# A hybrid decoder layer on one core: three token chunks in the first phase, value products of a chunk as one batch, masks in pairs

## The chip, the cores and the metric

The kernel runs on one core of a Trainium2 chip. The metric is the device time of one execution in microseconds (us); smaller is better. The core has a matrix engine (PE in the profile, with PEld for its weight loads), a vector engine (DVE), a scalar engine (ACT), a general engine (POOL), and a queue engine that issues most DMAs (SP). Matrix products land in eight banks of PSUM of 128 partitions by 512 floats; everything else lives in SBUF or in DRAM.

## The reference

One layer over a prompt of 2048 tokens (width 1024) and over 8 single-token decode requests. From the normalised input one projection of 3592 columns gives q, k, v (8 heads of 64), a forget gate per head, a gate za, and u, gv, zc of the spatial-gating group. Cut to what matters:

```python
h = rms_norm(x, g_norm);  p = h @ w_in
q, k, v, fz, za, u, gv, zc = split(p)          # q, k also RMS-normed per head
c = cumsum(log_sigmoid(fz + b_f))
s = q @ k.T * SCALE + c[t] - c[s]              # causal: s <= t, else -inf
attn = softmax(s) @ v
mix = tril(W_s) @ rms_norm(gv) + b_s           # inside chunks of 128 positions
y = x + concat(attn * silu(za), u * mix * silu(zc)) @ w_out
```

k, v and the log gates of the prompt are outputs too. The decode requests read paged caches of 512 positions. Products are in fp32 precision: most factors are split into a high and a low part of the reduced format fp32r, and three products (high*high, high*low, low*high) are summed.

## The kernel before

**First phase** (up to about 588 us). The prompt's normalised input is transposed and split; chunk `cp` of 512 tokens is four tiles of 2048 floats (`hh`, `hl`, 16 tiles over four chunks, from the pool `big` with 16 places). Eight units of weights follow each other. Units 0 to 4 (q, k, v, gates, gv) go over all 16 token tiles. Units 5 to 7 hold the weights of u, zc and za; they go over the first `NCP` chunks only, with two features at a time into the `acc` banks, 24 products of 512 columns for each feature and chunk. Meanwhile the decode requests' cache pages are read and scored. During unit 7 the first of the row maxima below are already made.

**Second phase** (to about 1169 us). `UNITS` is the list of (head h, chunk c of 512 queries). For each unit, `values` makes the transposed scores of every key tile kt of 128 keys (4c+4 of them): a product with `k1` (128 rows: high and low parts of k), one with `k2` (68 rows), both into a bank `sc`; the four tiles on the diagonal get a causal mask by a bf16 product of `identb` and `maskb` into the same bank between the two. ACT takes the exponential into a place `p` of `ring`; POOL (and DVE for some) adds the tiles up into `acc` for the softmax sum. The value products (`av` from `p` and `vst`, true fp32, 64 columns of the array, even key tiles in one half and odd ones in the other) are queued in `avq` and run when eight key tiles have been done (`AVB`) or the unit ends. A unit with c = 3 so has two batches of eight. At the end the two halves of `av` are added, stored (`aT`), and later `add_up` transposes the sums.

For a head, `maxima` runs ahead: products of `q1` and `k2` into banks `tp`, for each query tile i in pieces of up to 512 keys, the last piece with the same kind of mask product, then a DVE minimum (`mn`) of each piece. `load_queries` brings a unit's queries (`q2`) in five DMAs, six key tiles before the unit before it ends (`QLEAD`).

Between these, `fill` hands out *filler*: the u, zc, za products of the chunks that the first phase left out (`filler`, bank `fl`, 24 products a feature and chunk, with new weights from `fill_weights` for each feature), then `load_out_weights` and the output products. The dose is `FILL` times the estimated time of the work just issued, `FILL7` in the last three units. With `FILL` 0.50 the 24 feature-chunks (two chunks of 12 features) last into unit (6,3).

**Last phase**: the remaining output products, into the banks `sc` and `av`.

PE's order is written out by hand in the order of the Python code; `Pe.clock` adds up estimated PE time, and `later(ns, fn)` defers a step until that clock has moved on. The other engines run in the order of the framework's scheduler; each engine and the SP queue is strictly first in, first out. The PSUM banks of the second phase are `sc` 2 (`NSC`), `tp` 3, `av` 2 (`NAV`), `fl` 1; a tile of a tag takes the bank of an earlier tile of that tag, and its first product waits until that one was read out.

Of the kernel before, what the change touches and what calls it, by code (L numbers as in the profile page):

```python
# [19 lines left out]
P = 128  # L20
# [58 lines left out]
def hymba_step(ctx, tc, x_prompt, x_sample, cache_k, cache_v, cache_logf, page_table, g_norm, w_in,  # L79
# [712 lines left out]
    def filler():  # L792
        jobs = [(o + f * P, f) for f in range(4) for o in (OZA, OU, OZC)] if NCP < 4 else []
        nxt = first.pop()
        mxs = {}
        units = []
        for n, (o, f) in enumerate(jobs):
            units.append(nxt)
            if n + 1 < len(jobs):
                nxt = fill_weights(jobs[n + 1][0])  # L800
            if n + 2 >= len(jobs):
                continue
            unit = units.pop()
            while len(unit) < KT:
                yield -1
            for cp in range(NCP, 4):
                if n % 3 == 0:
                    yield from za_steps(unit, 0, f, cp, "fl")
                elif n % 3 == 1:
                    mxs[cp] = s2(t="mxu")  # L810
                    yield from u_steps(unit, 0, f, cp, "fl", mxs[cp])
                else:
                    yield from zc_steps(unit, 0, f, cp, "fl", mxs.pop(cp))
                yield 0
        while min(len(unit) for unit in units) < KT:
            yield -1
        for cp in range(NCP, 4):
            mx = s2(t="mxu")
            yield from u_steps(units[0], 0, f, cp, "fl", mx)
            yield 0  # L820
            yield from zc_steps(units[1], 0, f, cp, "fl", mx)
            if cp == 3:
                break
            yield 0
            while "k1" not in heads.get(NH - 1, {}):
                yield -1
            load_out_weights(0)
# [69 lines left out]
    def maxima(hd):  # L897
# [2 lines left out]
        nxt = qhi.pop() if qhi else load_hi(h, 0)  # L900
        for c in range(2):
            q = nxt
            for i in range(8 * c, 8 * c + 8):
# [4 lines left out]
                cut = pieces((i + 1) * P)  # L908
                if i % 4 == 0:
                    part = sm.tile([P, 4, len(cut)], F32, tag="mn", bufs=3, name=tname("mn"))  # L910
                for n, (c0, m) in enumerate(cut):
                    sp = bank("tp")[:, :m]
                    end = n == len(cut) - 1
                    mm(sp, q[:HD + 2, (i % 8) * P:(i % 8 + 1) * P], hd["k2"][:HD + 2, c0:c0 + m], True, not end,
                       max(m, 256) * 0.422)
                    if end:
                        mm(sp[:, m - P:], identb, maskb[:, 0], False, True, 56)
                    nc.vector.tensor_reduce(part[:, i % 4, n:n + 1], sp, axis=AX.X, op=ALU.min)  # L918
                    yield m * 0.422
                if i % 4 == 3:  # L920
                    shifts(h, i // 4, part)

    shifted = set()
# [22 lines left out]
            later(3500, store)  # L946
        later(SLAG, turn)

    avq = []

    def run_av(keep):
        while len(avq) > keep:
            avq.pop(0)()

    due = {}
    nt = [0]
    qload = {}
# [5 lines left out]
    def values(at):  # L963

        h, c = UNITS[at]
        hd, q, acc, st = heads[h], qload.pop((h, c)), accs[at % 2], {}
        for kt in range(4 * c + 4):
            if kt == max(0, 4 * c + 4 - QLEAD) and at + 1 < len(UNITS):
                qload[UNITS[at + 1]] = load_queries(*UNITS[at + 1])
            n0 = max(0, kt - 4 * c) * P  # L970
            ns = max(512 - n0, 256) * 0.422
            sp = bank("sc")
            ks = slice(kt * P, (kt + 1) * P)
            mm(sp[:, n0:], hd["k1"][:, ks], q[:, n0:512], True, False, ns)
            if kt >= 4 * c:
                mm(sp[:, n0:n0 + P], identb, maskb[:, 1], False, False, 56)
            mm(sp[:, n0:], hd["k2"][:HD + 4, ks], q[:HD + 4, 512 + n0:], False, True, ns)
            if kt == 0:
                flush(at % 2)
            p = ring[nt[0] % len(ring)]  # L980
            nt[0] += 1
            nc.scalar.activation(p[:, n0:], sp[:, n0:], AF.Exp, bias=zero1, scale=-1.0)  # L982
            if kt == 0 or kt == 2 and c:
                p0 = p
            elif kt == 1:
                if n0:
                    nc.gpsimd.memset(p[:, :n0], 0.0)
                    n0 = 0
                nc.gpsimd.tensor_tensor(acc, p0, p, op=ALU.add)
            elif kt == 3 and c:  # L990
                nc.vector.tensor_tensor(accd, p0, p, op=ALU.add)
            elif kt % 4 == 3 and kt < 4 * c:
                nc.vector.tensor_tensor(accd, accd, p, op=ALU.add)
            else:
                nc.gpsimd.tensor_tensor(acc[:, n0:], acc[:, n0:], p[:, n0:], op=ALU.add)  # L995
                if kt == 4 * c + 1:
                    nc.gpsimd.tensor_tensor(acc, acc, accd, op=ALU.add)

            def step(kt=kt, p=p, n0=n0, acc=acc, c=c, st=st, at=at):

                if kt == 0:
                    st["av"] = bank("av")
                av, fin = st["av"], kt == 4 * c + 3
                e = kt % 2
                mm(av[e * HD:(e + 1) * HD, n0:], hd["vst"][:, kt], p[:, n0:], kt < 2, kt >= 4 * c + 2,
                   (512 - n0) * 0.844)
                if fin:
                    t = s2(t="at")
                    nc.scalar.copy(t[:HD], av[HD:])
                    nc.vector.tensor_tensor(t[:HD], t[:HD], av[:HD], op=ALU.add)  # L1010
                    later(STLAG if h < NH - 2 else STLAST, lambda: nc.sync.dma_start(aT[h * HD:(h + 1) * HD, c * 512:(c + 1) * 512], t[:HD]))

                    def add_up():
                        pt = bank("tp")
                        for j in range(4):
                            transpose(pt[:, j * P:(j + 1) * P], acc[:, j * P:(j + 1) * P], ident)
                        rs = small(4)
                        nc.vector.tensor_reduce(rs, pt.rearrange("p (j k) -> p j k", j=4), axis=AX.X, op=ALU.add)
                        nc.vector.reciprocal(rs, rs)

                        def done():
                            pt = bank("tp")
                            transpose(pt[:4, :P], rs, ident)
                            t = s2(t="rt")[:4, :P]
                            nc.scalar.copy(t, pt[:4, :P])

                            def store():
                                nc.sync.dma_start(rT[h, c * 512:(c + 1) * 512].rearrange("(n p) -> n p", p=P), t)
                                if h % 2:
                                    later(STLAST, lambda: gate(h // 2, c))  # L1030
                            later(STLAG if h < NH - 2 else STLAST, store)
                        later(2000, done)
                    due[at % 2] = add_up
                    later(ACLAG, lambda: flush(at % 2, add_up))
            avq.append(step)
            if kt % AVB == AVB - 1 or kt == 4 * c + 3:
                run_av(0)
            yield 2 * ns + (512 - n0) * 0.844

    MT = 17408 * 0.422  # L1040
    VT = 17408 * 0.422 * 4
# [95 lines left out]
    def out_tiles():  # L1137

        gs = None
        for i in range(NT):  # L1140
# [13 lines left out]
                gs = decode_out()  # L1154
            if gs is not None and i < 12:
                next(gs, None)
            yield from out_products(i, **ins.pop(i), tags=("sc", "av") if last_phase[0] else ("fl", "fl"))

    mgen = all_maxima()
    mdone = [0.0]  # L1160
# [111 lines left out]
    for at, (h, c) in enumerate(UNITS):  # L1272
        if c == 0 and h < NH - 1:
            heads[h + 1] = load_keys(h + 1)
        if (h, c) == (DSTART, 0):
            Pe.decode, Pe.steps = Pe.clock, chain(decode_gate(), decode_attention())
        dose = FILL if at < len(UNITS) - 3 else FILL7
        for v in values(at):
            vdone += v
# [2 lines left out]
            while mdone[0] / MT < min(vdone / VT + AHEAD, NH):  # L1282
# [4 lines left out]
                mdone[0] += m  # L1287
                fill(m * dose)
                pump()
    run_av(0)  # L1290
    hold[0] = 0.0
    last_phase[0] = True
    for _ in fgen:
# [39 lines left out]
```

## Time and profile before

| | us |
|---|---|
| median of 3 runs (1343.99 to 1346.61) | 1346.32 |
| profiled execution, its own time | 1347.51 |
| its span, first to last instruction | 1345.8 |
| PE busy, weight loads busy | 1304.6, 1006.6 |
| DVE, POOL, ACT busy | 706.9, 574.6, 433.1 |

Mean granted clock of the matrix engine: 0.987. All products are recorded on one helper line (L174; transposes on L178), so groups are told apart by tile names: `acc` is the first phase, `sc<-q,k` scores, `tp<-k,q` maxima, `av<-p,vst` value products, `fl` filler, `sc<-wo,am` and `av<-wo,am` output. Ends of products are modelled and overlap the next one's start, so the price of a product is read from the distance between starts, not from its listed duration. Each value product of one key tile appears as two records.

### The profile page before, as it was taken

What the parts mean: (1) busy time and instruction counts of PE and PEld (TensorE: products, weight loads), DVE (VectorE), ACT (ScalarE), POOL (GpSimd) and SP (SyncE); (2) the same over time, 40 slices, a digit from 0 to 9 for tenths busy, and PEclk for the clock granted to TensorE, in tenths of its full rate; (3) what the DMA queues carried; (4) which work ended last, traced back from release to release, by engine and by line L of the source; (5) the groups of instructions that cost most, each with busy time, mean ns of one, the idle gap of its engine ahead of it and who ended that gap; (6) DMA issues with size and microseconds to landing.
All of it is one profiled execution on the core that took longest, in us unless ns stands there. A gap on an engine that the chain in (4) does not pass through costs nothing.

```text
span 1345.8 us, 19516 instructions
## 1 busy us (share of the span) xinstructions
PE 1304.6 (97%) x6544; PEld 1006.6 (75%) x6544; DVE 706.9 (53%) x1328; ACT 433.1 (32%) x781; POOL 574.6 (43%) x679
## 2 busy tenths in 40 slices
PE   6999999999999999999999999999999998999998
PEld 5999999999887877866666566666656664688877
DVE  4346654534678544266586555566565774322321
ACT  5542332222222111114453344434444456310100
POOL 3113343423223554416776666676757466400000
PEclk9999999999999999999998899999999998999999
DMA  6644353555113665634254854666375645463221
GB/s 217 188 119 112 87 142 116 155 140 158 52 48 99 187 184 148 159 97 127 78 138 85 181 138 126 177 182 169 95 192 135 172 119 196 135 238 117 107 77 49
DMA packets 170805, 183.09 MB, mean 136 GB/s; under 512 B 39402, under 2 KB 125866, under 8 KB 169138
## 3 DMA queue, kind: packets, MB, share of 16 engines
q1 hardware_dynamic: 166818, 173.08, 46.7%
q10 hardware_dynamic: 3488, 8.39, 1.6%
q8 instruction: 52, 0.85, 0.3%
q14 instruction: 47, 0.39, 0.1%
q0 software_dynamic: 400, 0.38, 0.1%
HBM read 121.53 MB, written 60.28 MB: 135 GB/s over the span
## 4 chain that ended last, share of the span: by engine, by line
PE 85%; DMA 6%; DVE 4%; ACT 2%; issue 1%; SPq 1%; POOL 1%; ACTq 0%; DVEq 0%; POOLq 0%
PE acc L174 36%; PE sc L174 15%; PE av L174 14%; PE fl L174 10%; PE tp L174 5%; PE tp L178 3%; PE pm L174 1%; DVE mn L918 1%; ACT p L982 1%; DMA xp<-in_x_prompt_dram 1%; DMA raw<-in_w_in_dram 1%; DMA q<-qk_hi 1%; DMA k<-qk_lo 1%; DMA q<-qk_lo 1%; DMA mrow<-mt 0%
## 5 line engine op out<-in xcount | busy, mean ns | idle before, releaser
L982 ACT ACTIVATE p<-sc,zero 128x512 f32<-128x512 f32 (+1 forms) x320 | 196.6, 623 | 173.9 <-PE sc L174 167.9
L995 POOL TENSOR_TENSOR acc<-acc,p 128x512 f32<-128x512 f32 (+3 forms) x184 | 194.1, 1055 | 125.2 <-ACT p L982 104.1
L918 DVE TENSOR_REDUCE mn<-tp 128x1 f32<-128x384 f32 (+6 forms) x320 | 186.9, 604 | 107.9 <-PE tp L174 105.6
L174 PE MATMUL acc<-wh,hh 128*128 128x384 f32 (+2 forms) x640 | 228.7, 357 | 0.0
L174 PE MATMUL acc<-wl,hh 128*128 128x384 f32 (+2 forms) x640 | 222.8, 348 | 1.0 <-DVE wl L256 0.9
L174 PE MATMUL acc<-wh,hl 128*128 128x384 f32 (+2 forms) x640 | 222.6, 348 | 0.6 <-DVE hl L248 0.6
L174 PE MATMUL sc<-q,k 128*128 128x512 f32 (+7 forms) x640 | 211.1, 407 | 10.6 <-ACT p L982 5.9
L174 PEld LDWEIGHTS sc<-q,k 128*128 128x128 f32 (+1 forms) x640 | 118.2, 197 | 35.3 <-ACT p L982 16.3
L174 PE MATMUL av<-p,vst 128*64 128x512 f32 (+3 forms) x640 | 135.4, 543 | 0.0
L174 PEld LDWEIGHTS acc<-wh,hh 128*128 128x128 f32 x640 | 120.7, 189 | 7.2 <-ACT hh L243 0.2
L174 PEld LDWEIGHTS acc<-wl,hh 128*128 128x128 f32 x640 | 120.9, 189 | 6.3 <-DVE wl L256 2.0
L174 PEld LDWEIGHTS acc<-wh,hl 128*128 128x128 f32 x640 | 120.3, 188 | 6.3 <-DVE hl L248 1.2
L174 PE MATMUL tp<-k,q 66*128 66x384 f32 (+6 forms) x320 | 120.3, 392 | 3.9 <-DVE mn L918 3.3
L236 POOL TENSOR_SCALAR sm<-sm 128x6 f32<-128x6 f32 (+3 forms) x84 | 20.3, 241 | 238.8 <-DVE sm L389 170.4
L174 PEld LDWEIGHTS av<-p,vst 128*64 128x64 f32 x640 | 47.9, 137 | 67.1 <-issue 57.6
L237 POOL TENSOR_TENSOR sm<-sm,mhalf 128x6 f32<-128x6 f32 (+3 forms) x84 | 89.6, 1067 | 6.7
L174 PE MATMUL sc<-wo,am 128*128 128x512 f32 x360 | 84.5, 390 | 0.0
L174 PE MATMUL av<-wo,am 128*128 128x512 f32 x360 | 84.2, 389 | 0.0
L174 PEld LDWEIGHTS tp<-k,q 66*128 66x128 f32 x320 | 61.2, 193 | 26.6 <-DVE mn L918 6.6
L174 PE MATMUL acc<-hh,wh 128*128 128x512 f32 x192 | 76.3, 397 | 4.9 <-DVE s L378 4.9
L174 PEld LDWEIGHTS av<-wo,am 128*128 128x128 f32 x360 | 67.5, 188 | 14.2
L174 PEld LDWEIGHTS sc<-wo,am 128*128 128x128 f32 x360 | 67.4, 188 | 14.1
(218 smaller groups left out, 2087.2 us busy)
## 6 DMA issues: line engine op xcount, KB each, us to landing
raw<-in_w_in_dram SPq DMA_DIRECT2D x40, 256.0 KB
kb<-in_cache_k_dram SPq DMA_DIRECT2D x32, 256.0 KB
k<-qk_hi SPq DMA_DIRECT2D x16, 512.0 KB
q<-qk_hi SPq DMA_DIRECT2D x64, 128.0 KB
vb<-in_cache_v_dram SPq DMA_DIRECT2D x32, 256.0 KB
g<-gm SPq DMA_DIRECT2D x16, 512.0 KB
xy<-in_x_prompt_dram SPq DMA_DIRECT2D x16, 512.0 KB
out_dram<-xy ACTq DMA_DIRECT2D x15, 512.0 KB
```

The costliest lines, as they stand in the source:

```text
L174: Pe.last = nc.tensor.matmul(out, lhsT, rhs, start=start, stop=stop).ins
L178: Pe.last = nc.tensor.transpose(out, in_, idn).ins
L236: nc.gpsimd.tensor_scalar(r, ss, inv_n, EPS, op0=ALU.mult, op1=ALU.add)
L237: nc.gpsimd.tensor_tensor(r, r, mhalf[:rows, :n], op=ALU.pow)
L918: nc.vector.tensor_reduce(part[:, i % 4, n:n + 1], sp, axis=AX.X, op=ALU.min)
L982: nc.scalar.activation(p[:, n0:], sp[:, n0:], AF.Exp, bias=zero1, scale=-1.0)
L995: nc.gpsimd.tensor_tensor(acc[:, n0:], acc[:, n0:], p[:, n0:], op=ALU.add)
```

## The change

- `NCP` 3: units 5 to 7 go over three chunks in the first phase, so the filler has one chunk (12 feature-chunks) instead of two; its dose `FILL` falls to 0.27.
- `values` handles the diagonal key tiles first, in two pairs, each pair with its two masks back to back, then the others one by one; all value products of the unit follow in one batch at its end. `AVB` and `avq` are gone. `NSC` is 3, `NAV` 1, and `ring` has 18 places instead of 10. The additions are the same in number, in the new function `sums`; those of the diagonal tiles come behind the first other tile's.
- `maxima` handles query tiles in pairs: the masked piece of the first is left open until that of the second, which is now made first of its tile; both masks follow back to back, then both minima.
- `load_out_weights(1)` is called at unit (6,1), `load_out_weights(0)` where the filler ends. The output products in the last phase use `sc` banks alone.

```diff
-NCP = 2
-FILL = 0.50
+NCP = 3
+FILL = 0.27
-AVB = 8
-NSC = 2
+NSC = 3
-NAV = 2
+NAV = 1
...
     def fillers():
         yield from filler()
-        load_out_weights(1)
+        load_out_weights(0)
...
+                for j, cut in zip((i, i + 1), (cuts[0], cuts[1][::-1])):
+                    for (c0, m) in cut:
...
+                        if end:
+                            ends.append((sp, m, j, n))
+                            if j > i:
+                                for (sp, m_, _, _) in ends:
+                                    mm(sp[:, m_ - P:], identb, maskb[:, 0], False, True, 56)
+                                for (sp, _, j_, n_) in ends:
+                                    nc.vector.tensor_reduce(part[:, j_ % 4, n_:n_ + 1], sp, axis=AX.X, op=ALU.min)
...
+        groups = [(4 * c, 4 * c + 1), (4 * c + 2, 4 * c + 3)] + [(kt,) for kt in range(4 * c)]
+        for kts in groups:
...
+            for kt, sp, n0, ns, ks in todo:
+                mm(sp[:, n0:], hd["k1"][:, ks], q[:, n0:512], True, False, ns)
+            for kt, sp, n0, ns, ks in todo if kts[0] >= 4 * c else ():
                 mm(sp[:, n0:n0 + P], identb, maskb[:, 1], False, False, 56)
+            for kt, sp, n0, ns, ks in todo:
+                mm(sp[:, n0:], hd["k2"][:HD + 4, ks], q[:HD + 4, 512 + n0:], False, True, ns)
...
-            avq.append(step)
-            if kt % AVB == AVB - 1 or kt == 4 * c + 3:
-                run_av(0)
+        av = bank("av")
+        for kt in range(4 * c + 4):
+            p, n0 = ps.pop(kt)
+            e = kt % 2
+            mm(av[e * HD:(e + 1) * HD, n0:], hd["vst"][:, kt], p[:, n0:], kt < 2, kt >= 4 * c + 2, (512 - n0) * 0.844)
...
+        elif kt == 0:
+            add(acc, ps[4 * c][0], ps[0][0])
+            for j in range(4 * c + 1, 4 * c + 4):
+                add(acc, acc, *ps[j])
...
-    for t in [s8(t="p"), s8(t="p"), s4(t="p")]:
+    for t in [s8(t="p") for _ in range(4)] + [s4(t="p")]:
...
+        if (h, c) == (NH - 2, 1):
+            load_out_weights(1)
```

What the order of instructions shows at three places (LDWEIGHTS rows are those of the bf16 mask products; the others load their weights unlisted).

PE, before, the first two diagonal tiles of head 0, chunk 2 (`sc` from `k1`, mask, `sc` from `k2`, filler, a maxima piece, the next tile):

```order
L174 MATMUL sc_6658<-q_1083_6374,k_983_5911 128x512
L174 LDWEIGHTS identb
L174 MATMUL sc_6658<-maskb,identb 128x128
L174 MATMUL sc_6658<-q_1083_6374,k_982_5908 128x512
L174 MATMUL fl_6549<-hh_632,fh_6163 128x512
L174 MATMUL fl_6549<-hl_633,fh_6163 128x512
L174 MATMUL fl_6549<-hh_632,fl_6164 128x512
L174 MATMUL tp_6667<-k_1066_6285,q_1098_6436 128x512
L174 MATMUL sc_6670<-q_1083_6374,k_983_5911 128x384
L174 LDWEIGHTS identb
L174 MATMUL sc_6670<-maskb,identb 128x128
L174 MATMUL sc_6670<-q_1083_6374,k_982_5908 128x384
```

PE, now, the end pieces of two query tiles and the second diagonal pair of the same unit:

```order
L173 MATMUL tp_6834<-k_1100_6621,q_1059_6455 128x320
L173 MATMUL tp_6836<-k_1100_6621,q_1059_6455 128x384
L173 LDWEIGHTS identb
L173 MATMUL tp_6834<-maskb,identb 128x128
L173 LDWEIGHTS identb
L173 MATMUL tp_6836<-maskb,identb 128x128
L173 MATMUL sc_6842<-q_1114_6698,k_1003_6147 128x256
L173 MATMUL sc_6843<-q_1114_6698,k_1003_6147 128x128
L173 LDWEIGHTS identb
L173 MATMUL sc_6842<-maskb,identb 128x128
L173 LDWEIGHTS identb
L173 MATMUL sc_6843<-maskb,identb 128x128
```

The 256 mask products stand alone before (128 of `tp`, 128 of `sc`) and in 128 pairs now.

PE, before, the first batch of value products of the same unit (head 0, chunk 2); the second, of four key tiles, follows 32 rows later:

```order
L174 MATMUL sc_6623<-q_1083_6374,k_982_5908 128x512
L174 MATMUL av_6628<-p_6154,vst_5914 64x512 x2
L174 MATMUL av_6628<-p_6155,vst_5914 64x512 x4
L174 MATMUL av_6628<-p_6156,vst_5914 64x512 x2
L174 MATMUL fl_6549<-hh_632,fh_6163 128x512
```

PE, now, the whole unit's value products:

```order
L173 MATMUL sc_6987<-q_1114_6698,k_1002_6144 128x512
L173 MATMUL tp_6993<-k_1100_6621,q_1131_6771 128x512
L173 MATMUL av_6996<-p_6583,vst_6150 64x512 x2
L173 MATMUL av_6996<-p_6579,vst_6150 64x512 x4
L173 MATMUL av_6996<-p_6580,vst_6150 64x512 x2
L173 MATMUL av_6996<-p_6582,vst_6150 64x512
L173 MATMUL av_6996<-p_6582,vst_6150 64x384
L173 MATMUL av_6996<-p_6582,vst_6150 64x256
L173 MATMUL av_6996<-p_6582,vst_6150 64x128
L173 MATMUL sc_7012<-q_1162_6902,k_1003_6147 128x512
```

Over the program there were 48 batches and are 32.

SP, before, around the first unit's query loads (`zT` stores the za gate, `q_1065` are the queries of unit (0,0)):

```order
L519 DMA zT<-sz_6135 128x512
L944 DMA mrow<-mt_6146 4x128
L519 DMA zT<-sz_6140 128x512
L944 DMA mrow<-mt_6146 4x128
L786 DMA raw_6165<-in_w_in_dram 128x4x128
L786 DMA raw_6167<-in_w_in_dram 128x4x128
L893 DMA q_1043_6190<-qk_hi 64x1024
L894 DMA q_1043_6190<-kx 2x1024
L882 DMA q_1065_6279<-qk_hi 64x512
L883 DMA q_1065_6279<-qk_hi 64x512
L884 DMA q_1065_6279<-qk_lo 64x512
L885 DMA q_1065_6279<-kx 2x512
```

SP, now (`sz_6569` is made from the very last product of the first phase; `q_1099` are the queries of unit (0,0)):

```order
L518 DMA zT<-sz_6564 128x512
L518 DMA zT<-sz_6569 128x512
L785 DMA raw_6592<-in_w_in_dram 128x4x128
L785 DMA raw_6594<-in_w_in_dram 128x4x128
L875 DMA q_1099_6615<-qk_hi 64x512
L876 DMA q_1099_6615<-qk_hi 64x512
L877 DMA q_1099_6615<-qk_lo 64x512
L878 DMA q_1099_6615<-kx 2x512
L879 DMA q_1099_6615<-mrow 2x512
```

The query loads stand behind the same store of the last za tile and the same two filler loads as before. On PE, 54 products (22 maxima pieces, 24 of filler, masks and transposes) stand between the last product of the first phase and the first score before; 14 stand there now, since 28 instead of 12 of the 34 early maxima pieces are made during the first phase.

More of the change, by code (lines that the diff above doesn't have):

```diff
@@ L902, in maxima @@
             q = nxt
-            for i in range(8 * c, 8 * c + 8):
+            for i in range(8 * c, 8 * c + 8, 2):
                 if i == 2:
@@ L947, in shifts @@
         later(SLAG, turn)
[L949 to L953, printed above, removed]
     due = {}
@@ L983, in values @@
[L983 to L986, printed above, removed]
+            for kt, sp, n0, ns, ks in todo:
+                p = ring[nt[0] % len(ring)]
+                nt[0] += 1
+                nc.scalar.activation(p[:, n0:], sp[:, n0:], AF.Exp, bias=zero1, scale=-1.0)
+                if c == 0 and kt == 1:
                     nc.gpsimd.memset(p[:, :n0], 0.0)
                     n0 = 0
[L989 to L1034, printed above, removed]
@@ L1289, in hymba_step @@
                 pump()
-    run_av(0)
     hold[0] = 0.0
```

101 lines of the change are left out of this document (67 added, 34 removed).

## The prediction

> **What bounds the kernel now.** I read the page's busy times and its chain first, to know which engine sets the end.
>
> ```profile
> span 1345.8 us, 19516 instructions
> PE 1304.6 (97%) x6544; PEld 1006.6 (75%) x6544; DVE 706.9 (53%) x1328; ACT 433.1 (32%) x781; POOL 574.6 (43%) x679
> PE 85%; DMA 6%; DVE 4%; ACT 2%; issue 1%; SPq 1%; POOL 1%; ACTq 0%; DVEq 0%; POOLq 0%
> ```
>
> PE is busy for 97% of the span and is 85% of the chain that ended last. So a change gains only what it takes out of PE's own row of products, or out of the 41 us in which PE idles, or out of lowered clock. Then the windows by stage, to see where that idle time lies.
>
> ```profile
> core 0: us, PE busy (x) PEld busy (x) DVE busy (x) ACT busy (x) POOL busy (x), PEclk, DMA share, GB/s
> 573.00:604.00 31.00, 29.30 (x126) 20.27 (x125) 19.50 (x42) 2.72 (x6) 4.02 (x8) 0.94 0.38 98
> ...
> 700.00:765.00 65.00, 59.21 (x264) 37.81 (x263) 40.49 (x68) 25.27 (x46) 42.31 (x47) 0.90 0.60 129
> 765.00:1040.00 275.00, 271.19 (x1368) 171.31 (x1367) 160.12 (x291) 122.11 (x218) 186.40 (x211) 1.00 0.58 153
> ...
> 1095.00:1169.00 74.00, 68.03 (x283) 37.40 (x281) 35.85 (x45) 37.77 (x65) 49.83 (x42) 0.91 0.50 157
> 1169.00:1346.00 177.00, 173.11 (x769) 140.17 (x768) 46.25 (x58) 14.71 (x17) 1.54 (x2) 1.00 0.36 124
> ```
>
> The long middle of the second phase (765 to 1040) idles 3.8 of 275 us. The lost time sits at the phase boundary (clock 0.94), at 700 to 765 (clock 0.90, 5.8 idle) and in the tail without filler (clock 0.91, 6.0 idle). So most of what can be won is the price of the products themselves: masks and the switches to value products.
>
> **The masks in pairs.** The timeline of PE, as starts, durations and names:
>
> ```profile
> 661.02 0.35 PE L174 MATMUL tp<-k,q 66*128 66x416 f32 x1
> 661.22 0.23 PE L174 MATMUL tp<-maskb,identb 128*128 128x128 bf16 x1
> 661.26 0.72 PE L174 MATMUL sc<-q,k 128*128 128x512 f32 x2
> 661.82 0.36 PE L174 MATMUL tp<-k,q 66*128 66x448 f32 x1
> 662.02 0.64 PE L174 MATMUL sc<-q,k 128*128 128x512 f32 x2
> 662.49 0.37 PE L174 MATMUL tp<-k,q 66*128 66x448 f32 x1
> ```
>
> The mask starts at 661.22 and the next product 0.04 later; but the two score products behind it take 0.56 to the next start (661.26 to 661.82), the same two without a mask ahead 0.47 (662.02 to 662.49). A lone mask costs 0.04 + 0.09 = 0.13 us. The change turns 256 lone masks into 128 pairs. No two masks stand back to back before, so the second one's price is unknown. Lower bound: its start step, 0.04, with the whole 0.09 paid once per pair; a 128-column product at the pace of a 512-column one (0.23) would be 0.06. Upper bound: nearly all of the lone price, 0.11. I take 0.06, since the 0.09 falls on the product that follows a mask, an fp32 one with other weights, and in a pair only one of those follows. Saved per pair 0.07, times 128: **-9.0 us**, ends -2.6 (0.02) and -11.5 (0.09).
>
> **One batch of value products a unit.** Around a batch of eight key tiles (16 records, of which the last six are a row of their own):
>
> ```profile
> 654.42 0.63 PE L174 MATMUL sc<-q,k 128*128 128x512 f32 x2
> 654.98 3.65 PE L174 MATMUL av<-p,vst 128*64 128x512 f32 x16
> 658.57 0.50 PE L174 MATMUL fl<-hh,fh 128*128 128x512 f32 x1
> 658.90 0.39 PE L174 MATMUL fl<-hl,fh 128*128 128x512 f32 x1
> ```
>
> ```profile
> 657.18 1.46 PE L174 MATMUL av<-p,vst 128*64 128x512 f32 x6
> ```
>
> The two scores ahead take 0.56 instead of 0.47 (+0.09), the first filler product behind 0.33 instead of 0.23 (+0.10), and the batch 3.59 where eight tiles at 0.43 are 3.44 (+0.15); 0.43 is the last row's step of 1.39 for three tiles less 0.10 for its end. A batch therefore costs 0.34 beyond its products, and 48 become 32: 16 x 0.34 = **-5.4 us**. The places `p` of a whole unit must now live until its end; `ring` has 18 for 16 of them, so two tiles of the next unit can be made before the batch has run. That batch comes ahead of the third in PE's order, so nothing waits for long: 0.
>
> By the Trainium skill, "TensorEngine Tiling (Array Packing)", Key Properties, a change of the tiling mode drains the engine and a change of tile alone does not. By that rule the batches (128*64) pay a switch, but the masks (128*128 like the scores) do not, pairs would save nothing, and the gain would be 9 us smaller. The mask rows above disagree: 0.09 behind a mask of the same mode.
>
> **Products moved into the first phase.** 12 feature-chunks of 24 products change from filler to `acc`. The chain has such a group as
>
> ```profile
> 354.60 5.47 PE acc L174 x24
> ```
>
> 5.47 / 24 = 0.228 us each, the same as filler's step above (658.90 is followed by products every 0.23). Moved, not saved: 0. The weights of those features no longer have to be read again for a second chunk: less work for SP and POOL, off the path: 0.
>
> **The phase boundary.** Around the last first-phase product (588.39 in PE's row, its za gate on ACT and then the stores and loads on SP):
>
> ```profile
> 588.13 1.38 ACT L489 ACTIVATE th<-acc,zero 128x512 f32<-128x512 f32 x2 [0.47 <-PE acc L174]
> 588.39 0.39 PE L174 MATMUL acc<-hh,wl 128*128 128x512 f32 x1
> ...
> 590.23 0.27 PE L178 MATMUL tp<-ident,mx 128*8 128x128 f32 x1 [1.26 <-DVE mx L934]
> ...
> 591.15 0.34 SPq L519 DMA_DIRECT2D zT<-sz  x1
> ...
> 591.91 1.02 SPq L786 DMA_DIRECT2D raw<-in_w_in_dram  x2
> ...
> 594.45 0.45 SPq L882 DMA_DIRECT2D q<-qk_hi  x1
> ...
> 596.71 0.25 SPq L886 DMA_DIRECT2D q<-mrow  x1
> ```
>
> SP's last za store goes 2.8 us after that last product T (588.39 to 591.15), because it waits for ACT and DVE; then two filler loads (to T+4.5), then the five query loads, which take 2.5 us to issue (594.45 to 596.96). Before, 54 products stood between T and the first score and covered this; what was lost is, from the window 573 to 604, 1.7 us idle and 0.06 x 31 = 1.9 us of clock, 3.6 together. Now 14 stand there, about 5 us with the waits for `mn` that they already have (1.26 above). SP is no faster: queries issued by T+7. Their landing lies between the start of the next thing (0) and the longest query transfer on the chain:
>
> ```profile
> 753.01 6.95 DMA q<-qk_lo
> ```
>
> I take 3, so the first score at T+10 and a wait of 5 us. Behind a wait the clock falls:
>
> ```profile
> 722.00:726.00 4.00, 2.43 (x7) 1.35 (x7) 4.00 (x8) 0.86 (x2) 0.36 (x1) 0.77 0.01 2
> 726.00:730.00 4.00, 4.00 (x11) 3.06 (x11) 3.11 (x8) 1.47 (x3) 4.00 (x6) 0.50 0.35 112
> ```
>
> ```profile
> 723.57 0.50 PE L174 MATMUL tp<-k,q 66*128 66x512 f32 x1 [2.33 <-DVE mn L918]
> ```
>
> A wait of 2.33 us was followed by 4 us at 0.50, 2 us lost. So 5 + 2 - 3.6 = **+3 us**, ends -1 (landing at once: 2 + 0.5 - 3.6) and +8 (landing 6.95, wait 9, clock 2).
>
> **Third score bank, fewer filler products between scores.** From the waits between 572 and 1170, and two groups:
>
> ```profile
> PEld sc L174 <- ACT p L982: 16.3, 34, 1.8
> ...
> PE sc L174 <- ACT p L982: 5.9, 10, 1.5
> ...
> PE tp L174 <- DVE mn L918: 3.3, 4, 2.3
> ```
>
> ```profile
> L918 DVE TENSOR_REDUCE mn<-tp 128x1 f32<-128x512 f32 (+4 forms) x304 | 177.9, 606 | 97.1 <-PE tp L174 94.8
> L993 DVE TENSOR_TENSOR accd<-accd,p 128x512 f32<-128x512 f32 x24 | 27.6, 1148 | 11.8 <-ACT p L982 11.6
> ```
>
> Score products wait 5.9 us for ACT's exponential to free a bank. A third bank lets PE run one key tile further ahead: **-4 us** of it, ends 0 and -5.9. `av` with one bank instead of two costs nothing: its readers have a whole unit. But with dose 0.27 instead of 0.50 about half the filler between two scores is gone. Then scores, and with them the maxima that share their pace, come closer together, and a `tp` bank must be read by a 606 ns minimum, now and then behind a 1148 ns `accd`, before the third piece after it. The pairs make it tighter: two banks are held open until both masks are through. In two places of before the filler is dense and thin:
>
> ```profile
> 866.00:940.00 74.00, 73.77 (x377) 46.37 (x376) 45.68 (x79) 32.51 (x58) 52.45 (x60) 1.00 0.66 176
> ...
> 968.00:1003.00 35.00, 33.73 (x176) 20.40 (x176) 20.21 (x43) 17.30 (x33) 20.68 (x24) 1.00 0.72 185
> ```
>
> PE idles 0.23 of 74 us in the first (0.3%), 1.27 of 35 in the second (3.6%). I take about 2% more idle, since part of the 1.27 was for query loads, over the some 410 us that scores fill between 604 and 1095: **+8 us**, ends 0 and +14 (the full 3.3%).
>
> **Query loads.** PE's 5.8 idle us between 700 and 765 hold one wait for queries, at the end of the 6.95 us transfer above. The lead of six key tiles now includes the whole batch of value products, 16 x 0.43 = 6.9 us where c = 3, so such loads have landed: **-3 us** with the clock behind it, ends 0 and -6.
>
> **At nothing:** the diagonal tiles first, whose four additions arrive together on POOL (4 x about 1 us) while the sum is needed only at the unit's end; output weights loaded earlier, on SP, ACT and DVE, hidden by PE's full row; the tail (1095 to 1169), which still has hardly any filler. If that cover goes, the tail's 6 idle us grow or shrink by 5 at most. The last phase, on three `sc` banks instead of two plus two: 0, as its 4 idle us in 177 are not waits for banks in the main.
>
> **The sum:** -9.0 - 5.4 + 3 - 4 + 8 - 3 = -10.4 us. The profiled execution took 1347.5 us (span 1345.8 plus 1.7 around it), 1.2 above the median of the runs shown, so 1337.1 there and **1336** as a median.
>
> **Rivals.**
> G, *the thin filler costs nothing*: for it, only 3.3 us of waits for `mn` in the whole second phase; against it, the thin window. The +8 goes: 1328; with masks, score banks and query loads at their better ends (2.5, 1.9, 3) 1320.6. So 1320 to 1328.
> M, *masks in pairs save nothing*, because each pays its own switch whatever is next to it. For it: no row shows two together. Then -10.4 + 9 = -1.4: 1345, or 1341 with 4 us of the other terms at their better ends. The Trainium skill's tiling rule above would give this case; with the row against it I leave it the 0.12 below.
> Q, *the first score waits 10 us or more* for queries behind the za store: for it, the 6.95 transfer; the sum ends 5 to 12 us higher, 1341 to 1348.
> V, *slower: DVE becomes the bound of the score stretches.* DVE is busy 160 of 275 us there (58%), far from full on average, but in a stretch with less filler it is dense with 606 ns minima that come in twos. If each of the 128 pairs of pieces makes PE wait 0.2 us for its `tp` bank, that is 128 x 0.2 = +25.6 instead of +8, so -10.4 + 17.6 = +7, 1353; from 0.15 us a pair (+19, sum about 0) on this decides the sign. Range 1350 to 1362. For it: three `tp` banks with two open at a time; against it: the thin window, where the waits for the minimum were few, 0.8 us in 35:
>
> ```profile
> PE tp L174 <- DVE mn L918: 0.8, 2, 0.6
> ```
>
> **How the numbers follow.** Forecast (1328 to 1342) 0.50; G 0.15; M 0.12; Q 0.07; V 0.16. About 0.2% (2.7 us) is what a measurement of this kernel can tell from no change: 1343.6 to 1349.0. Faster: forecast, G, two thirds of M and a third of Q, 0.75; same: the rest of M and Q, 0.09; slower: V, 0.16. The range of 1320 to 1349 leaves out V and whatever lies below G, together less than 0.2.
>
> **What the profile after would show.** Right: about 14 us fewer between starts in the sum of mask and value rows; the second mask 0.04 to 0.06 behind the first; value products in 32 rows of up to x32; a wait of some 5 us for `q` near 664 us (588 + 288 x 0.228 = 654 is the end of the first phase, T + 10 the first score), with clock near 0.5 behind it; waits of `sc` for ACT under 3 us, those of `tp` for `mn` at about 10. The forecast is wrong if the `tp` waits pass 20 us (V), if the product behind a second mask is late by 0.09 again (M), or if the new batch makes ACT or POOL late for `ring`.

## The result: 2.9% slower

The changed kernel takes 1386.28 us (median of 4, 1378.24 to 1387.44) against 1346.38: ratio 1.0286, interval 1.0252 to 1.0321. The forecast was 1336, with 1350 to 1362 as its slower rival. The profiled execution was the shortest of the four, 1378.24; the other three had a mean clock of 0.962 to 0.965 over spans of 1383.4 to 1385.4, so 48 to 53 us were lost to the clock in them. Idle time and clock below are those of the profiled execution. The page after, span, busy times and chain:

```profile
span 1376.2 us, 19387 instructions
PE 1309.4 (95%) x6544; PEld 1022.7 (74%) x6544; DVE 712.0 (52%) x1328; ACT 423.4 (31%) x781; POOL 583.7 (42%) x679
PE 84%; DMA 6%; DVE 5%; issue 2%; POOL 1%; ACT 1%; SPq 1%; ACTq 0%; POOLq 0%; DVEq 0%
```

PE is busy 4.8 us longer than before with the same 6544 products, and idles 66.8 us (1376.2 - 1309.4) instead of 41.2. The granted clock fell from 0.987 to 0.971: 39.9 us lost (1376.2 x 0.029) instead of 17.5. Take both off the span and 1269.5 us of work at full clock are left, where before had 1287.1. So the products did become 17.6 us cheaper, where 14.4 were forecast for masks and batches, and 25.6 us of idle time and 22.4 us of clock ate that and 30 us more. The windows say where:

```profile
core 0: us, PE busy (x) PEld busy (x) DVE busy (x) ACT busy (x) POOL busy (x), PEclk, DMA share, GB/s
...
657.00:668.00 11.00, 5.20 (x17) 3.37 (x17) 5.52 (x10) 1.16 (x2) 0.78 (x2) 0.69 0.72 170
668.00:765.00 97.00, 90.09 (x448) 59.12 (x447) 64.81 (x117) 43.89 (x83) 72.06 (x86) 0.94 0.49 117
765.00:1040.00 275.00, 259.21 (x1277) 163.99 (x1277) 174.89 (x310) 121.04 (x230) 206.26 (x232) 0.94 0.60 150
...
1187.00:1376.00 189.00, 181.25 (x794) 146.13 (x792) 49.82 (x61) 14.61 (x17) 3.86 (x4) 0.98 0.35 122
```

The stretch 765 to 1040, which before idled 3.8 us at full clock, now idles 15.8 at 0.94. No single place is to blame; the longest waits of PE between 640 and 1220 are spread over minima (`mn`), the shifts made from them (`mt`), output sums (`xy`) and loads:

```profile
PE tp L173 <- DVE mn L920: 7.2, 8, 3.8
PE tp L173 <- ACT mt L942: 6.1, 3, 5.1
PE tp L173 <- DVE mn L918: 5.7, 7, 1.7
PE fl L173 <- DVE xy L1130: 4.2, 1, 4.2
PE sc L173 <- DMA q<-qk_lo: 4.1, 1, 4.1
```

Added up by the engine waited for, that view has some 29 us for DVE, 8 for ACT and 8 for loads; in the kernel before (572 to 1170) it was 7, 7 and 4. So most of the new waits are for DVE.

One of them in full, DVE first, then POOL, then PE's product that waited, and the clock behind it:

```profile
922.46 4.33 DVE L1030 TENSOR_TENSOR accd<-accd,p 128x512 f32<-128x512 f32 x1
926.72 1.75 DVE L1093 SCALAR_TENSOR_TENSOR ga<-ga,gz 128x512 f32<-128x512 f32 x1
928.38 1.18 DVE L920 TENSOR_REDUCE mn<-tp 128x1 f32<-128x448 f32 x2
```

```profile
922.48 1.29 POOL L1030 TENSOR_TENSOR acc<-acc,p 128x512 f32<-128x512 f32 x1
923.72 1.30 POOL L781 TENSOR_TENSOR fl<-raw,fh 128x512 fp32r<-128x512 f32 x1
924.97 4.61 POOL L1030 TENSOR_TENSOR acc<-acc,p 128x512 f32<-128x512 f32 x3
```

```profile
929.05 0.77 PE L173 MATMUL tp<-k,q 66*128 66x480 f32 x1 [3.79 <-DVE mn L920]
```

```profile
927.00:935.00 8.00, 5.95 (x16) 2.45 (x18) 4.98 (x7) 0.69 (x1) 6.27 (x5) 0.57 0.58 146
```

While POOL goes from one operation to the next without a break, an `accd` on DVE, listed at 1.15 us on average, takes 4.33, and the `ga` behind it 1.75. The minimum behind both in DVE's queue starts at 928.38, the piece that needs its `tp` bank waits 3.79 us, and from 927 to 935 the clock is 0.57 on average. The Trainium skill, "SBUF — State Buffer", Terms, calls the port pair of DVE and GpSimd exclusive, the loser blocked for a whole instruction; the 4.33 us beside three POOL operations agree. Such long operations are not what is new, though: the 48 additions into `accd` take 51.8 us in all here, 46.4 in the kernel before and 51.1 in e9, one of the two fastest kernels below. What is new is that PE has less other work to do meanwhile.

The longest wait of the second phase has a cause that the forecast put at nothing, the output weights loaded earlier. ACT stands 5.18 us before the cast of a weight that has not landed, the copy `mt` behind it in ACT's queue is late, and PE waits 5.11 us:

```profile
1093.78 0.62 ACT L242 CAST wo<-raw 128x512 fp32r<-128x512 f32 x1 [5.18 <-DMA raw<-in_w_out_dram]
1094.30 0.25 ACT L942 COPY mt<-tp 8x128 f32<-8x128 f32 x1
1094.61 0.80 PE L173 MATMUL tp<-k,q 66*128 66x512 f32 x1 [5.11 <-ACT mt L942]
```

Half clock lies over it from 1091.21 to 1098.04. A wait of 3.2 to 4.4 us for `mt` near this place is also in e3, e6, e10, e11 and e12 below, with or without additions; e2, with the same loads and the order of before, has none over 0.5. No run moved these loads alone.

The steps of the change itself look as they should. A pair of masks in the maxima and a batch of sixteen key tiles:

```profile
754.91 0.40 PE L173 MATMUL tp<-k,q 66*128 66x512 f32 x1
755.15 0.29 PE L173 MATMUL tp<-maskb,identb 128*128 128x128 bf16 x2
755.25 0.71 PE L173 MATMUL sc<-q,k 128*128 128x512 f32 x2
755.79 0.60 PE L177 MATMUL tp<-ident,acc 128*128 128x128 f32 x4
```

```profile
859.91 6.65 PE L173 MATMUL av<-p,vst 128*64 128x512 f32 x32
866.50 0.67 PE L173 MATMUL sc<-q,k 128*128 128x512 f32 x2
```

The pair costs 0.10 to the next start and that product pair 0.54 instead of 0.47: 0.17 for two masks instead of 0.26. Over all full-clock places of the trace the median for pair plus the 512-column product behind it is 0.409, and 0.233 for the product alone; a single mask plus that product, read in the kernel before, is 0.357. That is 0.072 saved a pair, 9.2 us in all 128. The batch takes 6.59 us.

### The profile page after: what moved, and what is told of

The parts are those of the page before. It is cut to its first block, busy times and chain, and to the rows that moved or that the text cites. A ratio compares the mean times of both kernels' runs of the same rounds, so it can differ in the third digit from the quotient of the medians.

```text
span 1376.2 us, 19387 instructions
## 1 busy us (share of the span) xinstructions
PE 1309.4 (95%) x6544; PEld 1022.7 (74%) x6544; DVE 712.0 (52%) x1328; ACT 423.4 (31%) x781; POOL 583.7 (42%) x679
## 4 chain that ended last, share of the span: by engine, by line
PE 84%; DMA 6%; DVE 5%; issue 2%; POOL 1%; ACT 1%; SPq 1%; ACTq 0%; POOLq 0%; DVEq 0%
PE acc L173 41%; PE sc L173 21%; PE av L173 8%; PE tp L173 5%; PE fl L173 4%; PE tp L177 3%; DMA q<-qk_hi 2%; POOL acc L1030 1%; PE pm L173 1%; DMA xp<-in_x_prompt_dram 1%; DMA aT<-at 1%; DMA raw<-in_w_out_dram 1%; DVE mn L920 1%; DVE mn L918 1%; ACT p L984 1%
## 5 line engine op out<-in xcount | busy, mean ns | idle before, releaser
L984 ACT ACTIVATE p<-sc,zero 128x512 f32<-128x512 f32 (+1 forms) x320 | 189.2, 622 | 141.6 <-PE sc L173 139.0
L1030 POOL TENSOR_TENSOR acc<-acc,p 128x512 f32<-128x512 f32 (+3 forms) x184 | 206.8, 1124 | 20.9 <-ACT p L984 6.6
L173 PE MATMUL sc<-q,k 128*128 128x512 f32 (+7 forms) x640 | 198.2, 402 | 8.7 <-DMA q<-qk_lo 4.1
L173 PE MATMUL sc<-wo,am 128*128 128x512 f32 x720 | 164.0, 389 | 0.0
L173 PEld LDWEIGHTS sc<-wo,am 128*128 128x128 f32 x720 | 135.0, 188 | 28.3
L173 PEld LDWEIGHTS sc<-q,k 68*128 68x128 f32 (+1 forms) x640 | 114.4, 201 | 36.8 <-issue 11.5
L920 DVE TENSOR_REDUCE mn<-tp 128x1 f32<-128x320 f32 (+5 forms) x192 | 118.1, 630 | 45.0 <-PE tp L173 43.8
L173 PE MATMUL acc<-hh,wh 128*128 128x512 f32 x288 | 114.1, 396 | 4.2 <-DVE s L377 4.2
L173 PE MATMUL acc<-hl,wh 128*128 128x512 f32 x288 | 113.0, 392 | 0.0
L173 PE MATMUL acc<-hh,wl 128*128 128x512 f32 x288 | 112.8, 392 | 0.0
```

The lines of the kernel that those rows point to most:

```text
L173: Pe.last = nc.tensor.matmul(out, lhsT, rhs, start=start, stop=stop).ins
L920: nc.vector.tensor_reduce(part[:, j % 4, n:n + 1], sp, axis=AX.X, op=ALU.min)
L1030: eng.tensor_tensor(t[:, n0:], a[:, n0:], b[:, n0:], op=ALU.add)
```

## The experiments

Two theories at first: *cover* or *load* (thin filler, long score stretches and bursts leave DVE and POOL no slack, so their lateness stops PE), and mechanisms of single parts (*bursts* of additions, the one long *batch*). All medians stand against runs of the kernel before on the same chip, 1345.7 to 1346.9. "Work" is the span less idle time and lost clock, as above, all three from the one profiled execution of each kernel, whose time lies up to 9 us off the median; the clock is known to three digits, so lost clock and work are good to some 0.7 us; the rows below each experiment are its second phase, first score to last value product, in the columns of the windows above.

| kernel | us | ratio to before (95% interval) | idle | lost clock | work |
|---|---|---|---|---|---|
| before | 1346.4 | | 41.2 | 17.5 | 1287.1 |
| changed | 1386.3 | 1.0286 (1.0252 to 1.0321) | 66.8 | 39.9 | 1269.5 |
| e1 filler, batches as before | 1330.3 | 0.9888 (0.9867 to 0.9910) | 38.0 | 5.3 | 1283.6 |
| e2 before + thin filler | 1363.0 | 1.0131 (1.0105 to 1.0157) | 53.3 | 21.8 | 1286.4 |
| e3 additions spread | 1370.4 | 1.0191 (1.0165 to 1.0216) | 61.2 | 30.0 | 1274.2 |
| e4 four `tp`, two `sc` | 1378.9 | 1.0216 (1.0170 to 1.0263) | 64.8 | 49.9 | 1270.9 |
| e5 batches of eight | 1354.1 | 1.0068 (1.0045 to 1.0091) | 52.5 | 18.9 | 1279.9 |
| e6 no additions | 1347.3 | 1.0001 (0.9983 to 1.0018) | 55.5 | 17.5 | 1275.9 |
| e7 e1, all masks apart | 1321.8 | 0.9808 (0.9778 to 0.9838) | 29.9 | 7.9 | 1283.4 |
| e8 e1, additions spread | 1331.3 | 0.9880 (0.9850 to 0.9911) | 40.1 | 5.3 | 1283.7 |
| e9 e1, maxima masks apart | 1322.0 | 0.9820 (0.9796 to 0.9845) | 33.0 | 5.3 | 1281.6 |
| e10 changed, all masks apart | 1376.5 | 1.0223 (1.0197 to 1.0249) | 65.8 | 28.9 | 1281.3 |
| e11 no DVE additions | 1361.9 | 1.0112 (1.0083 to 1.0141) | 56.1 | 27.2 | 1277.9 |
| e12 few POOL additions | 1353.2 | 1.0052 (1.0029 to 1.0076) | 54.9 | 21.7 | 1276.8 |
| e13 thin filler, evened | 1347.4 | 1.0014 (0.9989 to 1.0038) | 48.5 | 12.1 | 1282.6 |
| e14 before + third `sc` bank | 1340.5 | 0.9952 (0.9934 to 0.9971) | 41.5 | 17.4 | 1281.4 |
| e15 e6, batches of eight | 1342.5 | 0.9973 (0.9946 to 1.0001) | 45.8 | 18.8 | 1277.6 |

**e1, filler and batches put back.** The single batch needs a ring of 18 places, for which there is room only once three chunks are done in the first phase, so both went together.

```diff
-NCP = 3
-FILL = 0.27
+NCP = 2
+FILL = 0.50
...
+            if pos % 8 == 0 or pos == 4 * c + 4:      # value products of the tiles so far
...
-    for t in [s8(t="p") for _ in range(4)] + [s4(t="p")]:
+    for t in [s8(t="p") for _ in range(2)] + [s4(t="p")]:
```

> The changed kernel with the filler (two chunks left over, dose 0.50, output weights loaded where they were) and the value batches of eight (ring of 10) put back; diagonal first, mask pairs, three score banks stay. Theory cover (half the filler between scores is gone, so lateness of DVE and ACT that was there before now stops PE, and the clock halves behind each stop): 1330 to 1342, below the kernel before by the mask pairs (9.2 us) and some score waits. Theory bursts (four diagonal additions at a stretch on POOL slow DVE's operations, up to 4.33 us for one accd): still 1360 or more. Theory batch (one value batch of up to 7 us holds ACT and DVE in line): as cover, 1330 to 1345.

1330.26 us, 1.1% below before. The loss is in these two parts and what they do to the rest:

```profile
604.00:1145.00 541.00, 526.81 (x2647) 343.15 (x2645) 342.40 (x588) 251.72 (x463) 377.91 (x396) 1.00 0.55 147
```

Same additions and minima as in the changed kernel (POOL 378, DVE 342 us), but in 541 us instead of 519, and the clock is whole.

**e2, thin filler alone in the kernel before.**

```diff
-NCP = 2
-FILL = 0.50
+NCP = 3
+FILL = 0.27
```

> The kernel before with only the filler changed: three chunks in the first phase, dose 0.27, output weights loaded at (6,1) and at the filler's end. Theory cover: 1370 to 1390, most of the 40 us. Theories bursts and batch: 1341 to 1352, as moved products cost the same and neither the order nor the batches change.

The loads of the output weights moved with it. 1363.0: 16 us slower, between the ranges of the theories. Its waits are not those forecast; PE waits for queries:

```profile
PE sc L174 <- DMA q<-qk_hi: 8.8, 2, 5.0
PE sc L174 <- ACT p L976: 5.4, 13, 1.1
PE sc L174 <- DMA q<-qk_lo: 4.8, 1, 4.8
```

13.6 us for queries, 4.8 of them at the first score, against 3.9 in the kernel before. As I read it, units are shorter, so the lead of six key tiles is a shorter time, and the loads take as long as they did; that was not tried by itself.

**e3, additions spread.**

```diff
         elif kt == 0:
             add(acc, ps[4 * c][0], ps[0][0])
-            for j in range(4 * c + 1, 4 * c + 4):
-                add(acc, acc, *ps[j])
+        elif kt == 1:
+            add(acc, acc, ps[1][0])
+            add(acc, acc, *ps[4 * c + 1])
+        elif kt == 2:
+            add(acc, acc, *ps[4 * c + 2])
...
```

> The changed kernel with the additions of diagonal tiles 2 to 4 made one each behind the off-diagonal tiles 1, 2 and 3 instead of all behind the first. Theory bursts: 1350 to 1370. Theories cover and batch: 1380 to 1390, no more than 6 us better.

1370.4, 16 us faster: the burst that the forecast put at nothing is real, but the smaller part.

**e5, batches of eight.** The loop of e1 with ring and filler of the changed kernel.

> The changed kernel with the value products in batches of eight key tiles (48 batches instead of 32), ring of 18 kept. Theory batch: 1355 to 1370, although 16 more batches cost 5.4 us. Theories cover and bursts: 1385 to 1395.

1354.1, 32 us faster although PE's own work rises by 10.4. The largest single effect.

```profile
666.00:1169.00 503.00, 476.08 (x2372) 298.49 (x2374) 329.82 (x574) 244.98 (x455) 376.97 (x398) 0.97 0.58 153
```

**e4, a fourth `tp` bank for the third `sc` bank.** `NSC = 2`, `NTP = 4`.

> The changed kernel with four tp banks and two sc banks instead of three and three. Theory load (with thin filler, long score stretches and bursts of additions, DVE and POOL fall behind the pace of scores and maxima, and three tp banks are too little slack): 1365 to 1380, less some 4 us of score waits. Theory latency (the stalls come from fixed delays, query loads, sums of minima, output weights, that shorter units no longer cover): 1385 to 1392.

1378.9, with single times from 1371.7 to 1387.7: inconclusive. The waits moved more than they went: in its profile, from 640 to 1220, PE waits 6.0 us for minima at `tp` instead of 12.9, but 12.6 us for ACT at `sc` instead of 0.9, so the bank taken away hides what the bank added does.

**e6, e11, e12: without additions.** e6 leaves out all additions but one scaled copy a unit, e11 DVE's, e12 168 of POOL's 240; the softmax sums are then incomplete, products and minima are all there.

> The changed kernel without the additions of the exponentials (one scaled copy a unit on POOL is left, so the softmax sums are left out): some 200 us of POOL and 30 of DVE are gone. Theory load: 1340 to 1355; what is left over 1330 are the wait at the first score and waits for queries. Theory latency: 1372 or more.

> The changed kernel without DVE's additions of the exponentials (48 of them, some 46 us of DVE; a quarter of the off-diagonal tiles is left out of the softmax sums), POOL's all there. If DVE's own load decides: 1350 to 1365. If POOL's stretches decide, by holding up DVE's operations or by what waits for POOL itself: 1375 or more.

> The changed kernel without POOL's additions of single exponentials (one scaled copy and the addition of DVE's sum are left in a unit; most tiles are left out of the softmax sums), DVE's all there. If POOL's stretches decide: 1348 to 1360. If DVE's own load decides: 1372 or more.

1347.3, 1361.9 and 1353.2: 39, 24 and 33 us faster than the changed kernel. So the load of the additions is what the change could not bear; both engines have part in it, and the two parts overlap (24 + 33 is more than 39). Both act through DVE: PE's waits for DVE between 640 and 1220, some 29 us in the changed kernel, are 20 in e11, 15 in e12 and 11 in e6, and for POOL itself it waits nowhere in that view. In e12 DVE has the same 1328 instructions and is busy with them for 675.7 us instead of 712.0, so POOL's additions lengthen DVE's work by 36 us. What e6 still waits for is of another kind:

```profile
PE sc L173 <- DMA q<-qk_hi: 12.0, 3, 6.6
```

**e15, e6 with batches of eight.**

> The kernel e6 (the changed kernel without the additions, so without softmax sums; 1347.3) with value batches of eight. Theory load (the one batch hurts because DVE and POOL then have to do their work in the shorter time of the scores): without that work eight gain little, 1340 to 1354 with 5.4 us for 16 more batches. If the one batch hurts by itself (what waits for its end, loads of queries issued in its shadow): 1318 to 1332, as 32 us less.

1342.5: only 4.8 us faster, where the same edit gave 32 with the additions. The one batch hurts through the load, not by its length. As I read it: between batches the changed kernel goes through up to sixteen key tiles with nothing but scores, maxima and thin filler on PE, and DVE has to keep up with that pace for all of them.

**e7, e9, e10: masks apart.** e7 is e1 with every mask alone, e9 the same for the maxima only, e10 the changed kernel with every mask alone.

```diff
-                            ends.append((sp, m, j, n))
...
+                            mm(sp[:, m - P:], identb, maskb[:, 0], False, True, 56)
+                            nc.vector.tensor_reduce(part[:, j % 4, n:n + 1], sp, axis=AX.X, op=ALU.min)
```

> The kernel e1 (filler and batches as before, 1330.3) with every mask product alone again, in scores and in maxima; order of tiles and banks as in e1. The price read in the profile of the changed kernel (0.409 us for a pair with the product behind it, 0.357 for a single mask with it, 0.233 for the product alone: 0.072 saved a pair, 128 pairs): 9.2 us more, 1338 to 1341. If the pairs save nothing by themselves: 1329 to 1332.

> The kernel e7 (1321.8, masks apart) with the masks of the scores in pairs again and those of the maxima alone. Theory maxima pairs (two of three tp banks stay open together and their two minima come in a row, so PE waits for DVE; score pairs only save): 1315 to 1320, e7 less some 5 us for 64 pairs. Theory score pairs (two score banks filled together make PE wait for ACT): 1324 to 1331.

> The changed kernel with all masks alone again, in scores and maxima. If pairs bunch the work of DVE and ACT here as in e1: 1355 to 1375. If their saving of 9 us is all that they do here: 1392 to 1397.

My expectation for e7 was the price read from the trace, and it failed in its sign: 1321.8, 8.5 us faster than e1 with its pairs. e9 with score pairs is the same, 1322.0. So pairs in the maxima cost 8 us net, pairs in the scores neither gain nor lose. The waits of PE in the second phase, e1 and then e9, show the maxima's part:

```profile
PE sc L173 <- ACT p L990: 3.5, 8, 0.8
PE sc L173 <- DMA q<-qk_hi: 2.3, 1, 2.3
PE tp L173 <- DVE mn L924: 1.8, 4, 1.1
```

```profile
PE sc L173 <- ACT p L986: 3.1, 7, 0.8
PE sc L173 <- DMA q<-qk_hi: 2.6, 1, 2.6
...
PE tp L173 <- DVE mn L920: 0.2, 1, 0.2
```

Those rows explain 1.6 us of the 8. The rest of it is in steps a little longer than their median all over the stretch (transposes into `tp` alone take 4.6 us less in e9, 46.3 against 50.9 from start to start over the whole execution), so that the saving of the pairs does not show in PE's work here: 1283.6 in e1, 1283.4 in e7; which of the two held banks or the two minima in a row does it was not tried. In the changed kernel, masks apart give 10 us by the medians (e10; single times of 1374.9 to 1377.7 against 1378.2 to 1387.4), although PE's work rises by 11.8.

**e8, spread additions on e1.**

> The kernel e1 (filler and batches as before, 1330.3) with the additions of the diagonal tiles spread over the next tiles as in e3. If the bursts cost only where filler is thin: 1328 to 1332. If they cost by themselves, as the 16 us of e3: 1315 to 1325.

1331.3, no different from e1: with thick filler and batches of eight the burst costs nothing.

**e13, thin filler with the bunching taken out** (batches of eight, maxima masks apart, additions spread; the score pairs stay).

> The changed kernel with its filler split kept, but everything that bunches work put back: value batches of eight, maxima masks alone, diagonal additions spread; score pairs stay. Theory load (each of them only hurts because DVE and POOL have no slack where filler is thin): what is left is the price of thin filler in itself, as in e2 (16.1 over its base) on the base of e9 (1322.0): 1335 to 1345. If the single gains (32, 16, 10) add up: 1322 to 1330. If they are the same gain taken in three ways: 1350 to 1356, no better than e5.

1347.4, just above what the load theory gave. The bunching costs 38.9 us under thin filler (1386.3 to 1347.4), less than the sum of the single gains (32 + 16 + 10): they take the same slack. The thin filler itself costs 25.4 against e9 (1322.0), which differs from e13 otherwise only in the spread additions, the larger ring and the place of the output weights' loads.

**e14, the third score bank alone.** `NSC = 3`, `NAV = 1` in the kernel before.

> The kernel before with three score banks and one for value products (output products in score banks), nothing else. The predicted term was 4 us of score waits: 1340 to 1345. If the third bank is what made e7 and e9 24 us faster than before: 1320 to 1328. If that came from the order (diagonal first): 1342 to 1348.

1340.5: 5.2 to 5.9 us (against 1345.7 or 1346.4), as forecast, and PE's waits for ACT at `sc` fall from 5.9 to 2.0 us. The other 18.5 us to e9 come with the rest of what is new there: the order of key tiles, additions and maxima pieces, and the score pairs, which e7 does without. In the two profiles e9 is 11 us ahead at the first score of unit (7,1) (1094.60 against 1105.25) and gains 10 more from there to the end; e14 waits 5.39 us for the last unit's queries, with half clock behind it, and e9 nowhere over 0.8 us after 800 us. Which part of it does this was not separated.

## Why the prediction was wrong, step by step

- **Masks in pairs, -9.0.** The price was right (0.072 a pair against 0.07), the rule of rival M did not hold, and PE's work fell (by 11.8 from e10 to the changed kernel). The step that failed is that nothing else follows from a pair: the maxima's pairs cost 8 us net in e9, all pairs together 10 in e10.
- **One batch a unit, -5.4.** The price was right again: 6.59 us for sixteen key tiles where the two batches before take 3.58 + 3.15 and 0.19 more around the second. "Nothing waits for long: 0" was wrong by 37 us (32 net in e5), and is the largest error. I asked whether `ring` would run out, and not what DVE and POOL did during the batches that went away.
- **Phase boundary, +3.** Right in mechanism, and too small: 7.5 by the same count, inside the ends. The last first-phase product and the first score, and the windows around them, before and now:

```profile
657.05 0.39 PE L173 MATMUL acc<-hh,wl 128*128 128x512 f32 x1
...
667.52 1.09 PE L173 MATMUL sc<-q,k 128*128 128x512 f32 x2 [4.08 <-DMA q<-qk_lo]
```

```profile
586.00:606.00 20.00, 18.30 (x75) 12.31 (x73) 16.20 (x34) 3.70 (x7) 4.02 (x8) 0.91 0.53 135
655.00:675.00 20.00, 14.20 (x59) 9.64 (x57) 7.47 (x13) 4.96 (x10) 4.47 (x9) 0.74 0.63 152
```

  T + 10.5 instead of T + 10. Idle time and lost clock are 5.8 + 5.2 = 11.0 now and 1.7 + 1.8 = 3.5 before. The term that was too small is the clock: 5 us where I took 2 from one window of 4 us. Half clock lasts from 661.14 to 671.38 here, and even behind the wait that I took the 2 from it lasted 6.83 us, so 3.4 were lost there. The chain before also has a query transfer of 8.26 us (from 1129.62), longer than the 6.95 that I called the longest.
- **Third score bank, -4.** Right: 5 to 6 in e14, with 3.9 us less of the waits that it was worked out from.
- **Thin filler, +8, ends 0 and +14.** e2 (16) and e13 (25) hold the phase boundary too, by the count above some 8 of e2's and 4 of e13's. What is left is 8 in e2, the size forecast, and 21 in e13, above the upper end. The kind was another: the working carried over the idle share of one thin window and nothing of the clock that each longer wait lowers, and it looked at minima where e2 waits for queries.
- **Query loads, -3.** No gain. The wait at 759 us before (2.46) is gone, but a new one of 2.80 stands at 1019.6, with half clock from 1019.53 to 1033.18 over and behind it. Behind the first score, waits for queries are 3.4 us now and were 3.9.
- **Output weights loaded earlier, nothing.** The wait of 5.11 us above, with 3.4 us of clock, stands behind such a load.
- **Diagonal additions, nothing.** Wrong by 16 us here (e3), right where there is filler (e8). I counted POOL's time, not DVE's beside it.
- **The rivals.** V had the mechanism, a late DVE in the score stretches, and the side, with a chance of 0.16; its price counted only waits for `tp` banks, and its range ended at 1362. Of the 48.0 us more of idle time and lost clock, 22.4 are clock.
- **The signs.** Those listed for a right forecast came: a pair at 0.10 for two masks, value products in 32 rows, a wait of 4.08 us for `q` before the first score, `sc` waits for ACT of 0.9 us and `tp` waits for minima of 12.9 (7.2 + 5.7), not over the 20 that would have spoken for V. The time was 50 us off all the same, because the signs looked at the steps that were priced and not at the sum of PE's waits.

The forecast's deepest fault was to add terms measured at a kernel with slack. The ledger in runs: thin filler with the phase boundary +25 (e9 to e13), bunching +39 (e13 to changed), all else -24 (before to e9).

## What to carry to other kernels

Before filler is taken away or batches are merged, look at what the other engines do in their shadow: an engine at 58% on average can be what the busiest one waits for where there is no cover, and the price of a step on the busiest engine says nothing of that. Where waits of 1.5 us or more are followed by half clock, as in the changed kernel, price them with it. The best version here keeps the thick filler, the batches of eight and the single maxima masks, and takes only the third score bank and the diagonal-first order: 1322 us (e7, e9), 1.8% below before.

## What the runs showed of the hardware

The clock fell behind shorter waits than I had reckoned with. A wait of 1.72 us in the changed kernel, and the clock 1.1 us later:

```profile
741.98 0.44 PE L173 MATMUL tp<-k,q 66*128 66x384 f32 x1 [1.72 <-DVE mn L918]
```

```profile
743.10:746.50 3.40, 3.40 (x13) 2.25 (x12) 1.92 (x4) 1.41 (x4) 3.40 (x8) 0.50 0.02 5
```

From 400 us on, every wait of PE of 1.5 us or more in the changed kernel has half clock over it or beginning within 2 us behind it. It is not so everywhere: behind waits of 2.60 (at 751.75) and 1.96 us (at 775.72) in e9 and of 2.88 us (at 777.60) in e2 the clock stayed whole; what makes the difference was not tried. Up to the last one, which the end of the execution cuts, half clock lasts 3.41 us or a multiple of it in all these traces, up to 13.65 in the changed kernel. And idle time does not show every wait: listed durations of products overlap the next start by some 0.17 us, so a wait below that shows in no idle time, only in the distance between starts.
